# A hybrid decoder layer on one core: the second norm summed across partitions by a product with ones, an earlier GLU input, a square root on ScalarE in the last norm, and sample rows stored in four pieces

## Chip, cores and metric

The kernel runs on one core of one Trainium2 chip. The metric is device time in microseconds (us), the median of several runs. Before the change it is 1431.86 us (three runs, 1431.58 to 1431.98).

## What is computed

One layer of a decoder over 256 prompt positions and 8 x 8 sample positions (320 columns in all), width 2048, all in float32:

```python
h = rms_norm(x, norm_mix)
u, q, k, v, g = split(h @ w_in)
y, s5_re, s5_im = s5_mixer(u, ...)            # complex diagonal scan, then gelu
y = y * sigmoid(y @ w_glu + b_glu)            # the GLU
o, ret_new = retention_chunked(rotary(q), rotary(k), v)
x = x + concat([y, silu(g) * group_norm(o)]) @ w_out
h2 = rms_norm(x, norm_ffn)                    # the second norm
gate, up = split(h2 @ w_ffn_in)
x = x + (silu(gate) * up) @ w_ffn_out
y_prompt, y_sample = rms_norm(x, norm_final)  # the last norm
```

with `rms_norm(x, g) = x * rsqrt(mean(x*x) + 1e-6) * g`. The states of the S5 part and of the retention are outputs too.

## The kernel before

Activations lie transposed: features on the 128 partitions, the N = 320 positions along the free dimension, so x is 16 tiles of 128x320. Every product with weights is made of three products in the fp32r format: weights and activations are split into a high part (a cast) and a low part (the rest), and hi*hi, hi*lo and lo*hi are added in one PSUM bank. `wload` (L132 to L135) fetches 128x1024 weights into `raw` on the SP queue, ACT casts them to `hi`, DVE subtracts to get `lo`; each of the three has three buffers. `gemm` (L145 to L147) runs the three products for each of the contraction's 128-row blocks. Results go to PSUM tiles with the tag "acc", of which there are three.

The order of instructions on PE and POOL is that of the program. Side work (norms, S5 chunks, heads) is written as generators that `spawn` puts on a heap with a due time; `gemm` runs the due ones between two blocks, by a clock `clk.now` that adds up costs written by hand. ACT, DVE and SP are ordered by a scheduler with priorities, except in the last part (`tail_order`), where they keep the program's order too.

The stages in question, in order of time:

- The output projection of the retention half: 16 products `ps_o` of the eight 128-row blocks in `r4a` and `r4b` (hi and lo of each head). `r4a` lies in the buffer "tab" of the S5 pool.
- The GLU: ACT halves the gelu's result `u32` into `yhi` (L1083), DVE takes the rest into `ylo` (L184), and eight products `ps_g` follow; ACT takes their sigmoid (L1098). `yhi` and `ylo` lie in the pool `glp`, which reuses the place of the S5 pool, that of `r4a` among it.
- The output projection of the GLU half (`ps_o2`). DVE adds each result to `x1`; ACT multiplies by the norm's weight into `hhi`, DVE makes `hlo`; squares are summed over the 16 tiles into `acc2` (128x320).
- The second norm, `ffn_norm`, which runs between the first products `ps_fg` of the FFN. `rstd_bcast` sums `acc2` over the partitions with products against a column of ones (positions on partitions, three columns), DVE finds the reciprocal root of the 128x3 numbers in eleven small steps (a guess from the bits, three Newton steps), three products with the identity spread it over all partitions, and ACT copies it from PSUM to `rbc2`. `ffn_in` multiplies each PSUM result by `rbc2`.
- The FFN: 88 products of 16 blocks (`ps_fg`, `ps_fu`) and 61 of 11 blocks (`ps_fo`).
- The tail, from L1336: the last three of the 16 feature tiles are computed with positions on partitions (128 + 128 + 64 rows x 384 features, `ps_t0`, `ps_t1`, `psa` with `psb`), so that the last norm's sum of squares comes from `accum_out` of one ACT Square (`chain`, L1312) plus the sum over the other 13 tiles (`sm3`). For each of the three position tiles `root_of` (L1298) finds the reciprocal root of one column on DVE: a sum, a guess from the bits, and three Newton steps of two instructions each. `bcast` (L1316) spreads it over the partitions with a product on PE, ACT copies it for POOL (`rbt`), DVE and POOL scale the 13 feature tiles (`scale`), ACT scales the 384 token-major features (`tok_out`), and SP or ACT issue the stores. `keep_warm(12)` (L1376) puts twelve unused products of 128x512 on PE between tile 1 and the last `bcast`.

Of the kernel before, what the change touches and what calls it, by code (L numbers as in the profile page):

```python
# [12 lines left out]
F32 = mybir.dt.float32  # L13
# [33 lines left out]
def hybrid_kernel(ctx, tc, xT, w_in, w_in4, w_out, w_glu, w_fi, w_fo, w_fot, gfr, vecs, s5p, bc, x0,  # L47
# [9 lines left out]
    def f(t):  # L57
        return t.bitcast(F32)
# [30 lines left out]
    def spawn(gen, delay=0.0):  # L89
        clk.n += 1  # L90
        heapq.heappush(clk.heap, (clk.now + delay, clk.n, gen))
# [91 lines left out]
    def stt(out, a, s, b, o1, o2):  # L183
        dve.scalar_tensor_tensor(out, a, s, b, o1, o2)  # L184
        return out
# [718 lines left out]
    def do_g(h):  # L904
        ps = proj(11 + 4 * h)
        sg = mp.tile([P, N], F32, name="sg", tag="sg", bufs=2)
        with tc.high_priority(offset=EVAC):
# [4 lines left out]
        run_due()  # L912

    DL = dict(b1=14.2, b2=6.6, scan=17.8, y=10.0, k=8.5, v=6.1,
              o=2.2, u=6.0, c=10.0, n2=2.4, n2b=2.6, nm=0.8)
    T0, PER = 53.6, 32.0


# [133 lines left out]

    rhi, rlo = Cols(), Cols()

    def split_r(t_, h):
        with tc.high_priority(offset=EVAC):
            act.copy(t_[:, 0], retp[:, h])
            tt(t_[:, 1], retp[:, h], f(t_[:, 0]), SUB)
        rhi.a.append(t_[:, 0])
        rlo.a.append(t_[:, 1])  # L1060
# [9 lines left out]
    for h in range(4, H):  # L1070
        while not ("sg" in HS[h] and "gn" in HS[h]):
            advance()
        split_r(r4b[:, h - 4], h)
    while clk.heap:
        advance()
    s5stack.close()
# [8 lines left out]
    for n in range(KT):  # L1085
        if n == 0:
            late = gemm_late("ps_o", lambda n: w_out[n, :, 8:16], 0, 4, 8, rhi, rlo)
        ps = late[n] if n < 2 else gemm("ps_o", w_out[n, :, 8:16], 8, rhi, rlo)
        tt(x1[:, n], x1[:, n], ps, ADD)
    rpool.close()  # L1090
# [44 lines left out]
        return ps_n.tile([P, 512], F32, name=name, tag="n", bufs=2)  # L1135

    def ffn_norm():
        rg = rstd_bcast(hp, acc2, norm_ps, "n2")
        next(rg)
        yield DL["n2b"]  # L1140
        act.copy(rbc2, next(rg))

# [34 lines left out]
    def ffn_in(c):  # L1179
        a = fp.tile([P, 2, FCT, N], F32R, name="ahl", tag="ahl", bufs=2)  # L1180
        for i in range(FCT):
            n = c * FCT + i
            if n == 0:
                spawn(ffn_norm(), DL["n2"])
            pg = gemm("ps_fg", w_fi[2 * n], KT, hhi, hlo)
            g = fp.tile([P, N], F32, name="fg", tag="fg", bufs=2)
            tt(g, pg, rbc2, MUL)
            act.activation(g, g, AF.Silu)
            if n == 0:
                wpool[:] = [wp2, WP2]  # L1190
            pu = gemm("ps_fu", w_fi[2 * n + 1], KT, hhi, hlo)
            u = fp.tile([P, N], F32, name="fu", tag="fu", bufs=2)
            tt(u, pu, rbc2, MUL)
            tt(u, u, g, MUL)
            act.copy(a[:, 0, i], u)
            tt(a[:, 1, i], u, f(a[:, 0, i]), SUB)
            if n >= 2:
                for _ in range(2 if n % 3 else 1):
                    states_step()
        return a  # L1200
# [97 lines left out]
    def root_of(i):  # L1298
        m = TILES[i][1]
        y_, t_, w_ = (a[0:m, i:i + 1] for a in (yy, th, wn))  # L1300
        ts(t_, rs[0:m, i:i + 1], sm3[0:m, i:i + 1], ADD, -0.5, MUL)
        ts(y_.bitcast(I32), t_.bitcast(I32), -0.5, MUL, float(0x1EF759DF), ADD)
        for _ in range(3):
            stt(w_, y_, t_, y_, MUL, MUL)
            stt(y_, w_, 1.5, y_, ADD, MUL)

    def chain(i, ps):

# [25 lines left out]
        q.dma_start(yp_o[i, :, a_:b_] if i < 2 else ys_o[:, a_:b_], outs[i][:, a_:b_])  # L1334

    with tail_order:  # L1336
        ps0 = ps_tok("ps_t0")
        mm3(ps0, 0, P, range(0, 5))
        pss = norm_ps("ps_s3")
# [44 lines left out]
        root_of(2)  # L1384
        pb2 = bcast(2)
        act.copy(rbt[0][:, 0:ms_], pb2[:, 0:ms_])
        scale(dve, 2, 0, 9, pb2)
        store(2, 0, 9)
        scale(pool, 2, 9, NF, rbt[0])
        tok_out(2, ts_o, act)  # L1390
        store(2, 9, NF)


def _host(inp):
# [99 lines left out]
```

## Time and profile before

| | us |
|---|---|
| median of 3 runs | 1431.86 |
| the profiled execution: device time | 1431.66 |
| its span, first to last instruction | 1429.9 |
| PE busy in the span | 1419.3 |
| DVE, ACT, POOL busy | 957.1, 602.9, 126.7 |
| first retention `ps_o` product, first GLU product, first FFN product | 343.9, 400.3, 485.4 |
| first product of the tail, last `bcast` | 1402.8, 1423.6 |

A row of the timeline reads: start, duration, engine, line of the kernel, operation, output<-input, shape, count, and in brackets the idle time of the engine before it and what ended it. A run of equal instructions is merged into one row with its count; products on PE overlap, so the step from one start to the next, not the duration, is what one costs the stream. Engine names with a q (SPq, ACTq) are the sequencers that issue DMAs. The chip's granted clock of TensorE is 0.999 in this execution.

### The profile page before, as it was taken

How to read it: one execution, taken by the hardware profiler on the slowest of the kernel's cores; microseconds unless marked ns; L12 is line 12 of the kernel's file. 1: busy time of each engine (PE TensorE's matmuls, PEld its weight loads, DVE VectorE, ACT ScalarE, POOL GpSimd, SP SyncE). 2: the span in 40 equal slices, each digit the busy share in tenths (PEclk: the TensorE clock that was granted, in tenths of full speed). 3: DMA queues.
4: the chain of work that ended last, by engine and by line, in shares of the span. 5: the costliest groups of instructions: out<-in, count | busy, mean ns of one | idle time of the engine just before them, and what ended most of it. 6: DMA issues, size and time to landing. Idle time of an engine off the chain costs nothing.

```text
span 1429.9 us, 26218 instructions
## 1 busy us (share of the span) xinstructions
PE 1419.3 (99%) x10386; PEld 1407.8 (98%) x10386; DVE 957.1 (67%) x1861; ACT 602.9 (42%) x959; POOL 126.7 (9%) x194
## 2 busy tenths in 40 slices
PE   9999999999999999999999999999999999999998
PEld 8999999999999999999999999999999999999997
DVE  7978887787567646776777545767744677655454
ACT  7645555554355533333333333333333333343452
POOL 7530022110000000000001000000000000000001
PEclk9999999999999999999999999999999999999999
DMA  8555555556444456675766446667445765455542
GB/s 287 173 171 164 162 170 160 168 165 207 161 154 151 158 206 225 221 255 197 250 201 235 136 147 241 235 208 246 159 151 178 256 232 179 156 169 174 161 129 74
DMA packets 102171, 267.07 MB, mean 187 GB/s; under 512 B 27360, under 2 KB 41888, under 8 KB 102048
## 3 DMA queue, kind: packets, MB, share of 16 engines
q1 hardware_dynamic: 101824, 265.04, 56.0%
q8 instruction: 81, 1.33, 0.4%
q10 hardware_dynamic: 224, 0.36, 0.1%
q14 instruction: 42, 0.34, 0.1%
HBM read 254.44 MB, written 10.52 MB: 185 GB/s over the span
## 4 chain that ended last, share of the span: by engine, by line
PE 71%; DVE 0%; issue 0%; POOL 0%; ACT 0%; POOLq 0%
PE ps_fu L146 7%; PE ps_fu L145 7%; PE ps_fu L147 7%; PE ps_fg L146 7%; PE ps_fg L145 7%; PE ps_fg L147 7%; PE ps_fo L146 7%; PE ps_fo L145 7%; PE ps_fo L147 7%; PE ps_o L146 1%; PE ps_o L145 1%; PE ps_o L147 1%; PE ps_t L1295 1%; PE ps_g L146 1%; PE ps_g L147 1%; PE ps_g L145 1%
## 5 line engine op out<-in xcount | busy, mean ns | idle before, releaser
L133 ACT CAST hi<-raw 128x1024 fp32r<-128x1024 f32 (+1 forms) x410 | 397.7, 971 | 681.2 <-PE ps_fg L146 184.2
L135 DVE TENSOR_TENSOR lo<-raw,hi 128x1024 fp32r<-128x1024 f32 (+1 forms) x410 | 463.2, 1130 | 307.3 <-ACT hi L133 304.4
L145 PE MATMUL ps_fg<-hhi,hi 128*128 128x320 f32 x704 | 217.5, 309 | 0.0
L146 PE MATMUL ps_fu<-hlo,hi 128*128 128x320 f32 x704 | 217.4, 309 | 0.0
L146 PE MATMUL ps_fg<-hlo,hi 128*128 128x320 f32 x704 | 217.4, 309 | 0.0
L147 PE MATMUL ps_fg<-hhi,lo 128*128 128x320 f32 x704 | 217.4, 309 | 0.0
L145 PE MATMUL ps_fu<-hhi,hi 128*128 128x320 f32 x704 | 217.4, 309 | 0.0
L147 PE MATMUL ps_fu<-hhi,lo 128*128 128x320 f32 x704 | 217.4, 309 | 0.0
L145 PE MATMUL ps_fo<-ahl,hi 128*128 128x320 f32 x671 | 207.4, 309 | 0.0
L146 PE MATMUL ps_fo<-ahl,hi 128*128 128x320 f32 x671 | 207.2, 309 | 0.0
L147 PE MATMUL ps_fo<-ahl,lo 128*128 128x320 f32 x671 | 207.2, 309 | 0.0
L145 PE MATMUL ps_p<-xhi,hi 128*128 128x320 f32 x560 | 177.3, 317 | 0.0
L147 PE MATMUL ps_p<-xhi,lo 128*128 128x320 f32 x560 | 173.0, 309 | 0.0
L146 PE MATMUL ps_p<-xlo,hi 128*128 128x320 f32 x560 | 172.8, 309 | 0.0
L146 PEld LDWEIGHTS ps_fg<-hlo,hi 128*128 128x128 f32 x704 | 132.4, 188 | 0.0
L145 PEld LDWEIGHTS ps_fg<-hhi,hi 128*128 128x128 f32 x704 | 132.4, 188 | 0.0
L145 PEld LDWEIGHTS ps_fu<-hhi,hi 128*128 128x128 f32 x704 | 132.4, 188 | 0.0
L146 PEld LDWEIGHTS ps_fu<-hlo,hi 128*128 128x128 f32 x704 | 132.4, 188 | 0.0
L147 PEld LDWEIGHTS ps_fu<-hhi,lo 128*128 128x128 f32 x704 | 132.4, 188 | 0.0
L147 PEld LDWEIGHTS ps_fg<-hhi,lo 128*128 128x128 f32 x704 | 132.3, 188 | 0.0
L146 PEld LDWEIGHTS ps_fo<-ahl,hi 128*128 128x128 f32 x671 | 126.2, 188 | 0.0
L145 PEld LDWEIGHTS ps_fo<-ahl,hi 128*128 128x128 f32 x671 | 126.2, 188 | 0.0
(480 smaller groups left out, 2119.7 us busy)
## 6 DMA issues: line engine op xcount, KB each, us to landing
raw<-w_fi SPq DMA_DIRECT2D x176, 512.0 KB, 4.2
raw<-w_in SPq DMA_DIRECT2D x79, 512.0 KB, 4.1
raw<-w_fo SPq DMA_DIRECT2D x61, 512.0 KB, 3.5
raw<-w_out SPq DMA_DIRECT2D x32, 512.0 KB, 3.7
hi<-vd SPq DMA_DIRECT2D x32, 512.0 KB, 5.6
lo<-vd SPq DMA_DIRECT2D x32, 512.0 KB, 5.3
raw<-w_fo SPq DMA_DIRECT2D x61, 192.0 KB, 2.4
rt<-r SPq DMA_DIRECT2D x8, 512.0 KB, 5.8
```

Source lines behind the costliest of these rows:

```text
L133: cast = act.copy(hi[:, :m], raw[:, :m])
L135: last_lo[0] = dve.tensor_tensor(lo[:, :m], raw[:, :m], f(hi[:, :m]), SUB)
L145: pe.matmul(ps, hi, xhi[:, k], start=k == 0, stop=False)
L146: pe.matmul(ps, hi, xlo[:, k], start=False, stop=False)
L147: pe.matmul(ps, lo, xhi[:, k], start=False, stop=k == nk - 1)
L1295: pe.matmul(ps[0:m, 0:TC], a3[:, x_, k, s:s + m], w_[:, k], start=k == 0 and x_ == 0 and w_ is whi, stop=k == FCT - 1 and w_ is wlo)
```

## The change

Four edits.

1. GLU input. The four heads in `r4a` are copied by ACT (two casts of 128x1280) into a new tile `r4c`, which the output projection reads from its fifth result on, so that the last reader of `r4a` comes after four results and not sixteen. The place that `yhi` and `ylo` share with it is free from then.
2. The second norm. `acc2` is split into high and low parts (`shi`, `slo`) on DVE, and two fp32r products with a 128x128 matrix of ones give the sum over the partitions on all partitions at once. DVE then computes the reciprocal root on the whole 128x320, in the same eleven steps, directly into `rbc2`. The six small products and the spreading ones, and ACT's copy, are gone. The due time is 3.4 instead of 2.4 + 2.6.
3. The last norm's root. ACT takes the square root, DVE the reciprocal, and one Newton step of two instructions follows instead of three. A first Sqrt on a column of ones stands at the head of the tail's program.
4. The sample rows. The nine feature tiles that DVE scales are scaled and stored as five and four, and the piece that POOL scales is stored by ACT's queue behind `ts_o`.

```diff
-              o=2.2, u=6.0, c=10.0, n2=2.4, n2b=2.6, nm=0.8)
+              o=2.2, u=6.0, c=10.0, n2=3.4, nm=0.8)
...
+    r4c = rpl.tile([P, 4, 2, N], F32R, name="r4c")
+    with tc.issue_after(last_r[0].ins):
+        for q in range(2):
+            act.copy(r4c[:, 2 * q:2 * q + 2], f(r4a[:, 2 * q:2 * q + 2]))
...
+        if n == 4:
+            rhi.a[0:4], rlo.a[0:4] = ([r4c[:, h, q] for h in range(4)] for q in range(2))
         ps = late[n] if n < 2 else gemm("ps_o", w_out[n, :, 8:16], 8, rhi, rlo)
...
     def ffn_norm():
-        rg = rstd_bcast(hp, acc2, norm_ps, "n2")
-        next(rg)
-        yield DL["n2b"]
-        act.copy(rbc2, next(rg))
+        shi, slo = (fp.tile([P, N], F32R, name=q, tag=q, bufs=2) for q in ("fg", "fu"))
+        ms, w = (hp.tile([P, N], F32, name=q, tag="sqx", bufs=2) for q in ("ms2", "rt2"))
+        with tc.high_priority(offset=2000):
+            dve.tensor_copy(shi, acc2)
+            tt(slo, acc2, f(shi), SUB)
+        yield DL["n2"]
+        ps = norm_ps("ps_r")[:, :N]
+        for i, a in enumerate((shi, slo)):
+            mm(0.15, ps, onesr, a, start=i == 0, stop=i == 1)
+        with tc.high_priority(offset=2000):
+            ts(ms, ps, -0.5 / D, MUL, -0.5 * EPS, ADD)
+            ts(rbc2.bitcast(I32), ms.bitcast(I32), -0.5, MUL, float(0x1EF759DF), ADD)
+            for _ in range(3):
+                tt(w, rbc2, rbc2, MUL)
+                tt(w, w, ms, MUL)
+                stt(rbc2, w, 1.5, rbc2, ADD, MUL)
...
-                spawn(ffn_norm(), DL["n2"])
+                spawn(ffn_norm())
...
     def root_of(i):
...
+        act.activation(w_, rs[0:m, i:i + 1], AF.Sqrt, bias=sm3[0:m, i:i + 1])
         ts(t_, rs[0:m, i:i + 1], sm3[0:m, i:i + 1], ADD, -0.5, MUL)
-        ts(y_.bitcast(I32), t_.bitcast(I32), -0.5, MUL, float(0x1EF759DF), ADD)
-        for _ in range(3):
-            stt(w_, y_, t_, y_, MUL, MUL)
-            stt(y_, w_, 1.5, y_, ADD, MUL)
+        dve.reciprocal(y_, w_)
+        stt(w_, y_, t_, y_, MUL, MUL)
+        stt(y_, w_, 1.5, y_, ADD, MUL)
...
     with tail_order:
+        act.activation(wn[:, 0:1], ones[:, 0:1], AF.Sqrt)
...
-        scale(dve, 2, 0, 9, pb2)
-        store(2, 0, 9)
+        scale(dve, 2, 0, 5, pb2)
+        store(2, 0, 5)
         scale(pool, 2, 9, NF, rbt[0])
         tok_out(2, ts_o, act)
-        store(2, 9, NF)
+        scale(dve, 2, 5, 9, pb2)
+        store(2, 5, 9)
+        store(2, 9, NF, act)
```

How this moves instructions, at three places. First DVE around the GLU's input, before (`ps_o` results are added to `x_4853`, which is `x1`; `u_119` is `u32`; `lo` splits weights):

```order
L135 TENSOR_TENSOR lo<-raw,hi 128x1024
L184 SCALAR_TENSOR_TENSOR ylo<-u_119,yhi 128x320 x5
L180 TENSOR_TENSOR x_4853<-x_4853,ps_o 128x320
L135 TENSOR_TENSOR lo<-raw,hi 128x1024
L184 SCALAR_TENSOR_TENSOR ylo<-u_119,yhi 128x320 x3
L135 TENSOR_TENSOR lo<-raw,hi 128x1024
L184 SCALAR_TENSOR_TENSOR sgl<-u_119,sgl 128x320
```

and after, where `y_4898` is the last S5 chunk's gelu input:

```order
L180 TENSOR_TENSOR y_4898<-y_4898,y_4897 128x320
L184 SCALAR_TENSOR_TENSOR u_119<-y_4898,y_4897 128x320
L180 TENSOR_TENSOR x_4853<-x_4853,ps_o 128x320
L135 TENSOR_TENSOR lo<-raw,hi 128x1024
L184 SCALAR_TENSOR_TENSOR ylo<-u_119,yhi 128x320 x7
L135 TENSOR_TENSOR lo<-raw,hi 128x1024
L184 SCALAR_TENSOR_TENSOR ylo<-u_119,yhi 128x320
L180 TENSOR_TENSOR x_4853<-x_4853,ps_o 128x320 x2
```

The eight `ylo` steps now follow the last S5 chunk, seven results of the projection earlier, and two additions of projection results wait behind them.

On ACT at the start of the projection and at the same place, after (before, `r4c` is absent, and the eight `yhi` stand as five and three on either side of the last weight cast but one ahead of the first sigmoid, L1098):

```order
L1079 CAST r4c<-r4a 128x1280 x2
L133 CAST hi<-raw 128x1024 x8
L689 ACTIVATE y_4898<-y_4897 128x320
L690 ACTIVATE y_4898<-y_4898,ones 128x320
L692 ACTIVATE y_4898<-y_4898 128x320
L133 CAST hi<-raw 128x1024
L1089 ACTIVATE yhi<-u_119 128x320 x8
L133 CAST hi<-raw 128x1024 x8
L1106 ACT_TABLE_LOAD
```

The two copies stand ahead of eight weight casts, the eight `yhi` directly behind the last gelu.

Second, DVE in the second norm, before (`acc_5783` is `acc2`, `ms`, `ry` and `rt` are the 128x3 tiles of the root):

```order
L180 TENSOR_TENSOR acc_5783<-acc_5783,sqx 128x320
L176 TENSOR_SCALAR ms<-ps_r 128x3
L176 TENSOR_SCALAR ry<-ms 128x3
L180 TENSOR_TENSOR rt<-ry 128x3
L180 TENSOR_TENSOR rt<-rt,ms 128x3
L184 SCALAR_TENSOR_TENSOR ry<-rt,ry 128x3
```

and after (`fg` and `fu` are the tiles of `shi` and `slo`, `ms_6415` and `rt_6416` the wide ones of the root, `rbc_5787` is `rbc2`):

```order
L180 TENSOR_TENSOR acc_5786<-acc_5786,sqx 128x320
L1149 CAST fg<-acc_5786 128x320
L180 TENSOR_TENSOR fu<-acc_5786,fg 128x320
L135 TENSOR_TENSOR lo<-raw,hi 128x1024
L176 TENSOR_SCALAR ms_6415<-ps_r 128x320
L135 TENSOR_TENSOR lo<-raw,hi 128x1024
L176 TENSOR_SCALAR rbc_5787<-ms_6415 128x320
L180 TENSOR_TENSOR rt_6416<-rbc_5787 128x320
L135 TENSOR_TENSOR lo<-raw,hi 128x1024
L180 TENSOR_TENSOR rt_6416<-rt_6416,ms_6415 128x320
L184 SCALAR_TENSOR_TENSOR rbc_5787<-rt_6416,rbc_5787 128x320
```

Of four splits of weights one stands ahead of the wide steps and two among the first of them; the last stands behind four more wide steps and ahead of the final two. The first multiplication by `rbc2` comes after all eleven. On PE the two products with ones stand behind 30 of the first 48 FFN products, the six sums of before stood behind 21 and the six spreading products behind 42.

Third, DVE at the last position tile, before:

```order
L180 TENSOR_TENSOR hi<-ps_b,ahl 64x384
L1330 TENSOR_TENSOR ahl<-x_4853,ps_b_15908 128x384
L176 TENSOR_SCALAR ahl<-ahl 64x1 x2
L184 SCALAR_TENSOR_TENSOR ahl<-ahl 64x1 x6
L1330 TENSOR_TENSOR ahl<-x_4853,ps_b_15952 128x576
```

and after:

```order
L180 TENSOR_TENSOR hi<-ps_b,ahl 64x384
L1350 TENSOR_TENSOR ahl<-x_4853,ps_b_15903 128x384
L176 TENSOR_SCALAR ahl<-ahl 64x1
L1323 RECIPROCAL ahl<-ahl 64x1
L184 SCALAR_TENSOR_TENSOR ahl<-ahl 64x1 x2
L1350 TENSOR_TENSOR ahl<-x_4853,ps_b_15944 128x320
L1350 TENSOR_TENSOR ahl<-x_4853,ps_b_15944 128x256
```

Of eight one-column steps on DVE four are left; the Sqrt is on ACT between the Square and the copy of `bcast`'s result. The table load for the Sqrt stands on ACT in the last FFN products, between the scaling of the last norm's weights (L1281 before) and that of its row form (L1282); no other load follows it.

More of the change, by code (lines that the diff above doesn't have):

```diff
@@ L1053, in hybrid_kernel @@
     rhi, rlo = Cols(), Cols()
+    last_r = [None]
     def split_r(t_, h):
         with tc.high_priority(offset=EVAC):
-            act.copy(t_[:, 0], retp[:, h])
+            last_r[0] = act.copy(t_[:, 0], retp[:, h])
             tt(t_[:, 1], retp[:, h], f(t_[:, 0]), SUB)
```

## The prediction, made before the changed kernel was run

> **What bounds the kernel now.** I read the page first, then the list of waits of PE, then the timeline of PE around each wait.
>
> ```profile
> PE 1419.3 (99%) x10386; PEld 1407.8 (98%) x10386; DVE 957.1 (67%) x1861; ACT 602.9 (42%) x959; POOL 126.7 (9%) x194
> ```
>
> PE is busy 99% of the span: the time is the stream of products, and only three things can shorten it: fewer products, fewer holes in their stream, and a shorter way from the last product to the end. All four edits lie at such places. The waits of PE name two of them:
>
> ```profile
> PE ps_b L1319 <- DVE ahl L184: 0.8, 2, 0.5
> ...
> PE ps_g L146 <- DVE ylo L184: 0.3, 1, 0.3
> ```
>
> The columns are the sum, the count and the longest: 0.8 us for the root in the tail, 0.3 for the GLU's `ylo`. These figures are taken from modelled ends of products, so I measure holes by steps between starts. "About what this kernel's measurement can tell" is 0.2%, 2.86 us.
>
> **Edit 1, the GLU input.** PE's timeline at the sixth block of the first GLU product:
>
> ```profile
> 402.54 0.31 PE L145 MATMUL ps_g<-yhi,hi 128*128 128x320 f32 x1
> 403.18 0.41 PE L146 MATMUL ps_g<-ylo,hi 128*128 128x320 f32 x1 [0.34 <-DVE ylo L184]
> 403.43 0.30 PE L147 MATMUL ps_g<-yhi,lo 128*128 128x320 f32 x1
> ```
>
> A product of 320 columns costs the stream 0.147 us (21 of them between the first two rows of the next fence: 3.08 / 21). Here two steps take 0.64 and 0.25: the hole is 0.89 - 0.29 = 0.60 us. With `ylo` made seven results of the projection earlier it closes: **-0.60**. What pays for it: two copies of 128x1280 and eight `yhi` that move on ACT, eight `ylo` that move on DVE.
>
> The copies: no row has that shape; the weight cast of 128x1024 in the next fence takes 1.05, and by its length 1280 columns take 1.3 each, 2.5 together with some overlap. They fit the idle 2.52 ahead of the cast that follows them:
>
> ```profile
> 349.40 1.05 ACT L133 CAST hi<-raw 128x1024 fp32r<-128x1024 f32 x1 [2.52 <-PE ps_o L164]
> ```
>
> Should they take longer, that cast (of the fourth result's weights) has cover: the product that needs it starts at 343.9 + 3 x 3.52 = 354.5 (24 steps of 0.147 are 3.52), and the cast and DVE's split are done 2.3 us after 349.4, so 2.7 us of lateness cost nothing. The eight `yhi` and `ylo` are some 3 to 4 us each, moved within a stage in which DVE and ACT have time:
>
> ```profile
> 343.90:400.30 56.40, 56.40 (x387) 56.34 (x385) 33.46 (x49) 21.54 (x30) 0.00 (x0) 1.00 0.60 205
> ```
>
> The columns are the stretch, then busy us of PE, PEld, DVE (33.46 of 56.40) and ACT (21.54). The two additions queued behind `ylo` come 3 us late, and their PSUM banks are wanted again two results (7.0 us) after they are full. So I price the cover at 0, with a bound of 0.6 above: then the hole has only moved.
>
> **Edit 2, the second norm.** PE's timeline from the first FFN product:
>
> ```profile
> 485.41 0.31 PE L145 MATMUL ps_fg<-hhi,hi 128*128 128x320 f32 x1
> ...
> 488.49 0.72 PE L104 MATMUL ps_r<-ones,acc 128*128 128x1 f32 x6
> 489.08 0.39 PE L145 MATMUL ps_fg<-hhi,hi 128*128 128x320 f32 x1
> 489.31 0.31 PE L146 MATMUL ps_fg<-hlo,hi 128*128 128x320 f32 x1
> ...
> 492.09 0.31 PE L147 MATMUL ps_fg<-hhi,lo 128*128 128x320 f32 x1
> 492.46 0.93 PE L104 MATMUL ps_r<-ident,ry 128*128 128x128 f32 x6
> 493.15 0.39 PE L145 MATMUL ps_fg<-hhi,hi 128*128 128x320 f32 x1
> 493.38 0.31 PE L146 MATMUL ps_fg<-hlo,hi 128*128 128x320 f32 x1
> ```
>
> The sums cost 489.31 - 488.49 - 0.147 = 0.67. The spreading products, the wait for `ry` ahead of them included, cost 493.38 - 492.09 - 2 x 0.147 = 1.00. Both go (1.67); two fp32r products of 320 columns come, 0.29: **-1.38**. Do they wait? The rows of DVE:
>
> ```profile
> 487.20 0.48 DVE L180 TENSOR_TENSOR acc<-acc,sqx 128x320 f32<-128x320 f32 x1
> ...
> 494.95 0.48 DVE L180 TENSOR_TENSOR fg<-ps_fg,rbc 128x320 f32<-128x320 f32 x1
> ```
>
> `acc2` is ready at 487.68; the cast and the subtraction, two steps of at most 0.49, end at 488.7. PE reaches the new products after 30 steps, 485.41 + 4.41 = 489.82: 1.1 us to spare.
>
> The root itself grows from eleven steps of 0.2 to eleven of up to 0.49, some 5.4 us, with three weight splits among them (1.2 each), and the last of those waits for this cast, which waits for PE:
>
> ```profile
> 497.73 1.05 ACT L133 CAST hi<-raw 128x1024 fp32r<-128x1024 f32 x1 [1.79 <-PE ps_fu L146]
> ```
>
> So `rbc2` is ready at about 500, not 493.9, and the first result is multiplied some 5 us later than at 494.95. What hides it: its bank is wanted by the fourth FFN product, three products of 7.04 us (48 steps) and 0.29 after 485.41, at 506.8, so 6 us are left; the splits that stand between the wide steps feed products that start 3 us or more after they end. ACT's copy leaves too, but ACT waits for nothing here. Cover gone would mean a wait of PE at 506.8; I price it at 0, bounds 0 and +1.
>
> **Edit 3, the root in the tail.** PE's timeline of the tail:
>
> ```profile
> 1412.27 0.34 PE L1295 MATMUL ps_t<-hlo,ahl 128*128 128x384 f32 x1
> 1412.57 0.49 PE L1319 MATMUL ps_b<-ident,ahl 128*128 128x128 f32 x2
> ...
> 1417.40 0.86 PE L1365 MATMUL ps_b<-hlo,ahl 128*64 128x384 f32 x4
> 1418.75 0.49 PE L1319 MATMUL ps_b<-ident,ahl 128*128 128x128 f32 x2 [0.48 <-DVE ahl L184]
> ...
> 1420.28 2.93 PE L118 MATMUL warm_ps<-ones 128*128 128x512 f32 x12
> 1423.55 0.40 PE L1319 MATMUL ps_b<-ident,ahl 64*128 64x64 f32 x2 [0.34 <-DVE ahl L184]
> ```
>
> A 384-column product steps by (0.86 - 0.34) / 3 = 0.173. So PE could have issued the first `bcast` at 1412.44 (0.13 lost), the second at 1417.40 + 4 x 0.173 = 1418.09 (0.66 lost). At the third the twelve warm products end, as modelled, 0.34 before it; with the overlap that the second shows (0.66 lost where 0.48 is listed) about 0.5 is lost. What the chain ahead of a `bcast` costs:
>
> ```profile
> 1416.72 0.19 ACT L1312 ACTIVATION_READ_ACCUMULATOR ahl<-hi 128x1 f32 x1
> 1417.60 0.48 ACT L1363 COPY ahl<-ps_a 64x384 f32<-64x384 f32 x1 [0.69 <-PE ps_a L1361]
> ```
>
> ```profile
> 1417.38 1.31 DVE L184 SCALAR_TENSOR_TENSOR ahl<-ahl 128x1 f32<-128x1 f32 x6
> ...
> 1420.48 0.55 DVE L180 TENSOR_TENSOR hi<-ps_b,ahl 64x384 f32<-64x384 f32 x1
> ```
>
> From the end of the sum of squares (1416.91) to the `bcast` (1418.75): 1.84. After: Sqrt, reciprocal and two steps of 1.31 / 6 = 0.22, with some 0.12 for four hand-overs, 0.56 and the two unknowns. The nearest rows for them:
>
> ```profile
> L922 ACT ACTIVATE warm<-ones 128x1 f32<-128x1 f32 x1 | 0.2, 203 | 0.0
> ```
>
> ```profile
> L432 DVE RECIPROCAL scrt<-scrt 128x32 f32<-128x32 f32 x1 | 0.4, 354 | 0.0
> ```
>
> The Sqrt lies between 0.20 (one column) and 0.48 (the copy of 384), the reciprocal between 0.20 (a one-column step) and 0.35 (32 columns); I take 0.25 and 0.20, both being one column. The chain is then 1.0, shorter by 0.8 (0.5 at the dear ends). Does PE collect it? First `bcast`: 0.13, all that PE lost. Second: 0.66 + 0.13 = 0.79 earlier, if the chain gives 0.66, which it does by 0.15. Then tile 2's sum (the row at 1420.48) waits for DVE, not PE: ACT's copy of `psa` at 1417.60 moves by 0.13 only, two additions and a scaling follow it on DVE, and the sum starts about 0.63 earlier. The chain ends 0.63 + 0.8 = 1.4 earlier, but PE is at the twelve warm products, which end 0.79 earlier, and so the last `bcast` comes 0.79 + 0.5 = about 1.25 earlier: **-1.25**. The warm products set it, with 0.15 to spare, so the dear ends cost 0.2 at most; the bounds are -0.9 and -1.4. Behind the Sqrt on ACT stands only the copy of `psa`, which waits for PE longer; behind the reciprocal on DVE stand tile 2's additions, which wait for that copy.
>
> The load of the Sqrt table costs what the sigmoid's does, 1.28 in the first row below, and falls into the hole of the last row, 2.42 in which ACT waits for a transfer:
>
> ```profile
> 405.57 1.28 ACT L1098 ACT_TABLE_LOAD   x1
> 406.86 0.53 ACT L1098 ACTIVATE sgl<-ps_g,vec 128x320 f32<-128x320 f32 x1
> ```
>
> ```profile
> 1342.56 0.53 ACT L1282 ACTIVATE ahl<-ahl 128x384 f32<-128x384 f32 x1 [2.42 <-DMA ahl<-gfr]
> ```
>
> 1.28 + 0.2 of the first Sqrt fit: 0.
>
> **Edit 4, the sample stores.** The rows of the two issuing queues, and of the transfers (KB each, time from issue to landing):
>
> ```profile
> 1424.78 0.56 ACTq L1326 DMA_DIRECT2D ts_o<-hi  x1
> 1425.01 1.06 SPq L1334 DMA_DIRECT2D ys_o<-ahl  x2
> ```
>
> ```profile
> rs_o<-raw SPq DMA_DIRECT2D x8, 512.0 KB, 6.7
> ...
> ys_o<-ahl SPq DMA_DIRECT2D x1, 128.0 KB, 3.4
> ts_o<-hi ACTq DMA_DIRECT2D x1, 96.0 KB, 3.0
> ```
>
> Before, the last piece is issued at about 1425.45 and lands 3.4 later, at 1428.8, 1.1 ahead of the span's end. After, by the same clock: five tiles scaled and issued 0.3 earlier (1424.7; 256 elements fewer, and 384 take 0.55 in the row at 1420.48), four at about 1425.15, and ACT's piece behind `ts_o`'s issue at about 1425.35. The last issue comes 0.1 earlier, and half of SP's bytes start 0.3 earlier: **-0.2**, bounds -0.5 and +0.4 (a fourth completion, a second issue of 0.5 on ACT).
>
> **Sum.** -0.60 - 1.38 - 1.25 - 0.2 = -3.43. The profiled execution is 1431.66, 0.20 under the median of 1431.86, and 1.76 longer than its span; I subtract from the median: **1428.4 us**, 0.24% faster.
>
> **The rivals.**
>
> *A hidden step shows, and the gain is within 0.2%.* A copy into `r4c` that takes the time of two casts and more, or a wide root step in the second norm that pushes a split past its product, puts a wait of 0.6 to 1 back; or the tail's stores land 0.5 later. Against it: every cover above is over a microsecond, except the tail's 0.15. For it: the forecast clears 2.86 by only 0.6. Time 1429.2.
>
> *The table set.* If Square is not served by the set that holds Sqrt, each tile's Sqrt is preceded by a load. Each chain becomes 2.3 instead of 1.84: 0.5 lost at each of the first two `bcast`, and at tile 2 another 0.3 for loading Square's set back (ACT is idle 1.01 there, below) and 0.5 for the Sqrt. With 0.1 to 0.2 back from the stores the tail ends 1.6 later: 1431.86 - 1.98 + 1.6 = 1431.5.
>
> ```profile
> 1421.06 0.53 ACT L1379 ACTIVATE ahl<-hi 64x384 f32<-64x384 f32 x1 [1.01 <-DVE hi L180]
> ```
>
> Against it: the program holds a single load for Sqrt, and Square and Copy have run behind the loads for Silu and Sigmoid without one of their own. The Trainium skill, "ScalarE: Activation LUTs", section "Table sets: the hidden batching unit", advises to group calls by table set, which speaks against mixing Sqrt with Square in one chain; it calls copy and identity members of every set and does not list Square. The Trainium skill's section "What ACT_TABLE_LOAD costs" gives 2.66 us for a switch (1283 ns of load and a drain of 1380); the load agrees with the row of this trace, where the sigmoid starts 1.29 after the load with no drain between. By the Trainium skill's price this rival would end near 1437.
>
> *Slower, by the stores.* The last 128 KB piece is now behind another on ACT's queue. A store of 512 KB lands after 6.7 us in this trace, under load. If the new last piece took that long from its issue (1425.35 - 1.25 + 6.7 = 1430.8, against 1428.8), the end would come 2.0 later than before and undo edits 1 and 2: 1431.9. From a landing of 6.6 on, the change is no gain, and past 9.5 us it is slower by 0.2%. Against it: the piece is a quarter of that size, and nothing else is under way.
>
> *No effect of edit 1.* If the scheduler's earlier `yhi` waited for something else that shares the place (the S5 outputs), the hole stays: 1429.0. The table of moved rows speaks against it.
>
> **Chances.** The forecast 0.68; a hidden step shows 0.2; edit 1 void 0.05; the table set 0.03; the stores 0.04. The 80% range takes the bounds of the four terms (-3.9 to -2.1, the latter with one cover gone): 1427.9 to 1429.8. Faster by over 0.2% is below 1429.0: 0.62 of the forecast's 0.68, and 0.06 of the second case, 0.68. Slower by over 0.2% takes both of the last two at their dear ends: 0.03. Within: 0.29.
>
> **What would show it.** In the changed profile: no wait of `ps_g` on `ylo`, and steps of 0.147 through the first GLU product; two products `ps_r` 4.4 us behind the first FFN product, 0.29 in all, and no wait at the fourth; the second `bcast` directly behind four `ps_b` products; the last one directly behind the twelve warm products, no longer listed as waiting for DVE; one Sqrt of about 0.25 and a reciprocal of about 0.2 in each chain; a last landing 1.4 to 1.5 earlier relative to the tail's first product. I am wrong if PE waits for `lo` after 343.9, 376 or 494, if a second table load stands in the tail, or if ACT's store lands over 4 us after its issue.

## The result, and the profile after

The changed kernel takes 1428.14 us (median of 9 runs, 1427.61 to 1428.76); the kernel before, run beside it, 1431.77 (9 runs, 1430.89 to 1432.89). The ratio is 0.9974, with a 95% interval of 0.9966 to 0.9983: 3.6 us faster, forecast 3.43. The interval ends at 0.17%, so the whole times alone leave open whether the gain is over 0.2%; the stages below make it 3.67 us, 0.26%. The span of the profiled execution went from 1429.9 to 1426.0.

The first row is the page's busy time of the changed kernel, in the form shown for the kernel before; the fence behind it is the whole list of waits of PE.

```profile
PE 1416.9 (99%) x10376; PEld 1406.4 (99%) x10376; DVE 958.0 (67%) x1852; ACT 606.4 (43%) x965; POOL 124.6 (9%) x194
```

```profile
PE warm_ps L118 <- POOL ones L64: 1.1, 1, 1.1
PE pss L104 <- POOL ksp L882: 0.9, 1, 0.9
PE py L953 <- ACT hi L943: 0.6, 1, 0.6
PE py L104 <- DMA toe<-toe: 0.5, 1, 0.5
PE py L953 <- DVE xhi L180: 0.3, 1, 0.3
```

The two waits that the prediction started from, `ps_b` on DVE and `ps_g` on DVE, are gone, and no wait stands in their place: all five rows left belong to the first 344 us, which no edit touches. PE's busy time fell by 2.4 us, with ten products fewer; the rest of the gain is time in which PE waited, or behind its last product, and 0.19 is an earlier first `ps_o` (343.91 and 343.72), which is no gain of the edits.

Where the time went is best read in stages, each from the start of one product of PE to the start of another, so that one execution's early or late start does not matter (us; the last column ends at the span's end, 1429.88 and 1426.03; the expectations further down have it from the span as rounded on the page, 6.35 and 5.92):

| | first `ps_g` to first `ps_fg` (edit 1) | first `ps_fg` to first `ps_fu` (edit 2) | first tail product to last `bcast` (edit 3) | last `bcast` to the end (edit 4) |
|---|---|---|---|---|
| before | 85.07 | 8.70 | 20.70 | 6.33 |
| after | 84.48 | 7.35 | 19.35 | 5.95 |
| difference | -0.59 | -1.35 | -1.35 | -0.38 |
| forecast | -0.60 | -1.38 | -1.25 | -0.2 |

The two long stages between are the same within 0.07 (56.43 and 56.50 from `ps_o` to `ps_g`, 908.74 and 908.68 from `ps_fu` to the tail). The four differences make -3.67.

**Edit 1.** ACT's timeline of the changed kernel at the start of the projection and behind the last gelu, then the group of `ps_g`'s products that read `ylo` (shortest, middle and longest duration in ns):

```profile
346.62 2.42 ACT L1079 CAST r4c<-r4a 128x1280 fp32r<-128x1280 f32 x2
349.24 1.05 ACT L133 CAST hi<-raw 128x1024 fp32r<-128x1024 f32 x1 [0.20 <-PE ps_o L164]
...
376.59 2.99 ACT L1089 ACTIVATE yhi<-u 128x320 fp32r<-128x320 f32 x8
```

```profile
L146 PE MATMUL ps_g<-ylo,hi x64: 309/309/309, 400.4 to 428.1; 128*128 128x320 f32 x64
```

The copies take 2.42 for both, and the weight cast behind them still waits for PE, 0.20 in the bracket where 2.52 stood: they fill the idle time, and the cast starts 5.52 us behind the first `ps_o`, against 5.49 before. All 64 `ylo` products now have the same duration; the longest took 412 ns before.

**Edit 2.** PE and then DVE of the changed kernel around the second norm:

```profile
488.95 0.31 PE L147 MATMUL ps_fg<-hhi,lo 128*128 128x320 f32 x1
489.11 0.31 PE L104 MATMUL ps_r<-fg,ones 128*128 128x320 f32 x1
489.25 0.31 PE L104 MATMUL ps_r<-fu,ones 128*128 128x320 f32 x1
489.40 0.32 PE L145 MATMUL ps_fg<-hhi,hi 128*128 128x320 f32 x1
```

```profile
487.44 0.49 DVE L180 TENSOR_TENSOR fu<-acc,fg 128x320 fp32r<-128x320 f32 x1
...
489.60 0.49 DVE L176 TENSOR_SCALAR ms<-ps_r 128x320 f32<-128x320 f32 x1 [0.53 <-PE ps_r L104]
...
498.36 0.49 DVE L184 SCALAR_TENSOR_TENSOR rbc<-rt,rbc 128x320 f32<-128x320 f32 x1
498.89 0.49 DVE L180 TENSOR_TENSOR fg<-ps_fg,rbc 128x320 f32<-128x320 f32 x1
```

Two products with ones stand in the stream at its usual step, 4.41 us behind the first FFN product (484.70). Their second input was ready at 487.93, 1.2 before PE came. The root on DVE ends at 498.85, 14.15 us behind the first product, and no product waits for it.

**Edit 3.** The tail of the changed kernel on PE, then the chain of the second tile on ACT and DVE, and the last step of the third tile's chain:

```profile
1410.35 0.38 PE L1339 MATMUL ps_b<-ident,ahl 128*128 128x128 f32 x2
...
1415.09 0.86 PE L1386 MATMUL ps_b<-hlo,ahl 128*64 128x384 f32 x4
1415.78 0.39 PE L1339 MATMUL ps_b<-ident,ahl 128*128 128x128 f32 x2
...
1417.22 2.92 PE L118 MATMUL warm_ps<-ones 128*128 128x512 f32 x12
1420.08 0.43 PE L1339 MATMUL ps_b<-ident,ahl 64*128 64x64 f32 x2
```

```profile
1414.40 0.18 ACT L1332 ACTIVATION_READ_ACCUMULATOR ahl<-hi 128x1 f32 x1
1414.62 0.29 ACT L1321 ACTIVATE ahl<-ahl 128x1 f32<-128x1 f32 x1
```

```profile
1414.95 0.16 DVE L1323 RECIPROCAL ahl<-ahl 128x1 f32<-128x1 f32 x1
1415.14 0.41 DVE L184 SCALAR_TENSOR_TENSOR ahl<-ahl 128x1 f32<-128x1 f32 x2
...
1419.33 0.40 DVE L184 SCALAR_TENSOR_TENSOR ahl<-ahl 64x1 f32<-64x1 f32 x2
```

The second `bcast` stands directly behind the four `ps_b` products (4 x 0.173 = 0.69), the third directly behind the twelve warm products; neither has a bracket any more. The Sqrt takes 0.29 and the reciprocal 0.16, and from the end of the sum of squares (1414.58) to the end of the last step (1415.55) it is 0.97. The old chain needed 1.84 to the `bcast` itself, of which 0.06 lay behind the last step (1418.69 to 1418.75), so 1.78 is the figure to compare: 0.81 less, forecast 0.8. The table load lies in ACT's hole, of which 0.88 is left:

```profile
1338.07 1.28 ACT L1357 ACT_TABLE_LOAD   x1
1339.36 0.20 ACT L1357 ACTIVATE ahl<-ones 128x1 f32<-128x1 f32 x1
1340.45 0.53 ACT L1302 ACTIVATE ahl<-ahl 128x384 f32<-128x384 f32 x1 [0.88 <-DMA ahl<-gfr]
```

**Edit 4.** The issues of the sample rows on the two queues of the changed kernel:

```profile
1421.30 0.55 ACTq L1346 DMA_DIRECT2D ts_o<-hi  x1
1421.94 0.54 ACTq L1354 DMA_DIRECT2D ys_o<-ahl  x1
```

```profile
1421.30 0.81 SPq L1354 DMA_DIRECT2D ys_o<-ahl  x2
```

The first feature-major piece is issued 1.22 us behind the last `bcast` (1.46 before), the last issue ends 2.40 behind it (2.5 before). The stage is 0.38 shorter, more than the earlier last issue gives; the store experiments below tell why.

### The profile page after: what moved, and what is told of

It is laid out like the page before. It is cut to its first block, busy times and chain, and to the rows that moved or that the text cites. A ratio compares the mean times of both kernels' runs of the same rounds, so it can differ in the third digit from the quotient of the medians.

```text
span 1426.0 us, 26198 instructions
## 1 busy us (share of the span) xinstructions
PE 1416.9 (99%) x10376; PEld 1406.4 (99%) x10376; DVE 958.0 (67%) x1852; ACT 606.4 (43%) x965; POOL 124.6 (9%) x194
## 4 chain that ended last, share of the span: by engine, by line
PE 76%; DVE 1%; issue 0%; ACT 0%; DMA 0%; SPq 0%; DVEq 0%; ACTq 0%
PE ps_fu L146 7%; PE ps_fg L146 7%; PE ps_fg L145 7%; PE ps_fu L145 7%; PE ps_fg L147 7%; PE ps_fu L147 7%; PE ps_fo L146 7%; PE ps_fo L145 7%; PE ps_fo L147 7%; PE ps_o L145 2%; PE ps_o L147 2%; PE ps_o L146 2%; PE ps_t L1315 1%; PE ps_g L147 1%; PE ps_g L145 1%; PE ps_g L146 1%
```

## The experiments

Eleven more kernels ran, and the changed one once more. Whole times of one kernel scatter by 1 to 3 us, and a single edit is worth 0.4 to 1.4, so the single edits are judged by the stages and the whole times are given beside them.

### Each edit alone

Four kernels are the kernel before with one edit each:

```diff
# edit 1 alone
+    last_r = [None]
...
-            act.copy(t_[:, 0], retp[:, h])
+            last_r[0] = act.copy(t_[:, 0], retp[:, h])
...
+    r4c = rpl.tile([P, 4, 2, N], F32R, name="r4c")
+    with tc.issue_after(last_r[0].ins):
+        for q in range(2):
+            act.copy(r4c[:, 2 * q:2 * q + 2], f(r4a[:, 2 * q:2 * q + 2]))
...
+        if n == 4:
+            rhi.a[0:4], rlo.a[0:4] = ([r4c[:, h, q] for h in range(4)] for q in range(2))
# edit 2 alone: ffn_norm and its due times as in the change
-        rg = rstd_bcast(hp, acc2, norm_ps, "n2")
...
+        for i, a in enumerate((shi, slo)):
+            mm(0.15, ps, onesr, a, start=i == 0, stop=i == 1)
...
# edit 3 alone: root_of and the first Sqrt as in the change
...
+        act.activation(w_, rs[0:m, i:i + 1], AF.Sqrt, bias=sm3[0:m, i:i + 1])
...
+        dve.reciprocal(y_, w_)
...
# edit 4 alone
-        scale(dve, 2, 0, 9, pb2)
-        store(2, 0, 9)
+        scale(dve, 2, 0, 5, pb2)
+        store(2, 0, 5)
...
-        store(2, 9, NF)
+        scale(dve, 2, 5, 9, pb2)
+        store(2, 5, 9)
+        store(2, 9, NF, act)
```

Edit 1: 

> Edit 1 alone, on the kernel before. Theory (PE's stream sets the time, each edit closes its own hole): no wait of ps_g on ylo, the stretch from the first GLU product to the first FFN product 0.60 us shorter (85.07 to 84.47), nothing else moved: 0.6 us faster, some 1431.2. Rival (the hole only moves: the copies or the late additions make PE wait elsewhere in the projection): same time as before, with a new wait of ps_o between 343 and 400 us.

Edit 2: 

> Edit 2 alone, on the kernel before. Theory: first ps_fg to first ps_fu 7.34 us instead of 8.70, no later wait of PE: 1.38 us faster, some 1430.4. Rival (the wide root on DVE holds back weight splits or the PSUM bank, and PE pays part of it later): under 0.8 us faster, with a wait of ps_fu or ps_fg between 492 and 510 us.

Edit 3: 

> Edit 3 alone, on the kernel before. Theory: from the tail's first product to the last bcast 19.35 us instead of 20.70 (1.35 less: 0.1, 0.65 and 0.6 at the three), and the end follows one to one: 1.3 us faster, some 1430.5. Rival (the end is set by the transfers of tile 1's stores or by POOL, not by the last root): the last bcast is 1.35 earlier but the span only 0.5 or less.

Edit 4: 

> Edit 4 alone, on the kernel before. Theory: last bcast where it was, first sample piece issued 0.3 us earlier, last one 0.1 earlier, landing 0.2 to 0.4 earlier: span 0.2 to 0.4 us shorter. Rival A (completion is fixed by the number of transfers): no gain or a loss up to 0.4. Rival B (this edit carries the gain that the sum did not foresee): 0.5 us or more.

| | edit 1 stage | edit 2 stage | edit 3 stage | edit 4 stage | first `ps_o` at | median, runs | ratio to before, 95% interval |
|---|---|---|---|---|---|---|---|
| before | 85.07 | 8.70 | 20.70 | 6.33 | 343.91 | 1431.97, 33 | |
| edit 1 alone | **84.48** | 8.70 | 20.70 | 6.31 | 343.35 | 1431.54, 11 | 0.9996 [0.9987, 1.0005] |
| edit 2 alone | 85.07 | **7.34** | 20.73 | 6.32 | 344.98 | 1430.96, 11 | 0.9993 [0.9984, 1.0002] |
| edit 3 alone | 85.07 | 8.70 | **19.33** | 6.32 | 344.66 | 1430.66, 11 | 0.9989 [0.9980, 0.9998] |
| edit 4 alone | 85.08 | 8.70 | 20.70 | **5.94** | 345.05 | 1431.93, 11 | 0.9999 [0.9990, 1.0007] |

Each edit moves its own stage by what it moves in the whole change, and no other stage of the table by more than 0.03. The four gains, 0.59, 1.36, 1.37 and 0.39, add up to 3.71 (3.67 in the whole change): they are independent. The stretch from the first `ps_o` to the first `ps_g` is not in the table; with edit 1 alone it is 56.58, against 56.43 before. The excess is time lost between `ps_o` products 3.6 to 3.8 us behind the first, up to 0.16 in one profile. Five of the ten profiles with `r4c` show none of it, and the kernel before has 0.06 of it, so it is at most a small part of what edit 1 gains. The whole times alone would not have told this: three of four intervals hold 1, because each edit is worth less than the 1.7 us by which the first `ps_o` moves between executions.

### Which of the two sets the last `bcast`: nine warm products instead of twelve

```diff
-        keep_warm(12)
+        keep_warm(9)
```

> The changed kernel with 9 instead of 12 warming products of 128x512 behind the second tile's sum product. In the changed kernel the last scalar product of the tail (1420.08) stands right behind the last warming product, and its input, scaled by ACT and DVE, was ready at 1419.73. If the warming products set the end there, as the prediction's working says, three fewer (about 0.24 each) uncover the chain of the last tile: the stage from the first tail product to the last scalar product goes from 19.35 to about 19.0, and the end comes 0.35 earlier. Rival: the chain itself, not the warming products, sets the end, and the stage stays at 19.35. Second rival: without the products PE's granted clock falls and the last products get longer by more than the 0.35, so the stage is 19.4 or more.

PE of this kernel, then DVE's last step ahead of the third `bcast`:

```profile
1418.67 2.25 PE L118 MATMUL warm_ps<-ones 128*128 128x512 f32 x9
1421.32 0.40 PE L1339 MATMUL ps_b<-ident,ahl 64*128 64x64 f32 x2 [0.40 <-DVE ahl L184]
```

```profile
1420.77 0.40 DVE L184 SCALAR_TENSOR_TENSOR ahl<-ahl 64x1 f32<-64x1 f32 x2
```

The stage went from 19.35 to 19.14, with the granted clock still at 1.00. Now the `bcast` waits for the chain, whose last step ends at 1421.17; the hand-over to PE takes another 0.15. So the twelve products do set the end in the changed kernel, by 0.21. I had expected 0.35, from the end of the chain without the hand-over. The whole time, 1428.52 (ratio 0.9975 [0.9967, 0.9984]), can't show 0.2.

### The cover of the wide root: eight Newton steps instead of three

```diff
-            for _ in range(3):
+            for _ in range(8):
                 tt(w, rbc2, rbc2, MUL)
```

> The changed kernel with 8 Newton steps for the second norm's root instead of 3: 15 more wide DVE instructions of about 0.52, 7.9 us in all, behind the sums and ahead of the scale of fg and fu; the values are the same but for rounding. It measures the cover that the prediction gave the root (the two bounds were 4.9 by the weight tile's low half on DVE and 6.7 by the PSUM bank of ps_fg that PE wants back). If that cover is right, PE waits 1.2 to 3 us behind the first product of the second weight product, and the time rises by that much against the changed kernel: 1429.3 to 1431.2. Rival: the root is on PE's path already and the whole 7.9 shows (1436). Second rival: DVE has more room than that and nothing shows (1428.1).

DVE at the end of the root, then PE at the fourth FFN product, which wants the bank back that the first result fills, then PE's clock by stretches (in front of the DMA share, the granted clock):

```profile
511.16 0.49 DVE L184 SCALAR_TENSOR_TENSOR rbc<-rt,rbc 128x320 f32<-128x320 f32 x1
511.69 0.49 DVE L180 TENSOR_TENSOR fg<-ps_fg,rbc 128x320 f32<-128x320 f32 x1
```

```profile
507.85 0.31 PE L147 MATMUL ps_fg<-hhi,lo 128*128 128x320 f32 x1
512.32 0.61 PE L145 MATMUL ps_fu<-hhi,hi 128*128 128x320 f32 x1 [4.16 <-DVE fg L180]
512.73 0.47 PE L146 MATMUL ps_fu<-hlo,hi 128*128 128x320 f32 x1
...
515.53 0.31 PE L145 MATMUL ps_fu<-hhi,hi 128*128 128x320 f32 x1
```

```profile
508.00:512.30 4.30, 0.16 (x2) 0.01 (x1) 4.13 (x9) 2.42 (x3) 0.00 (x0) 0.96 0.93 312
512.30:515.00 2.70, 2.68 (x10) 2.70 (x11) 1.79 (x4) 1.24 (x3) 1.91 (x1) 0.50 1.02 408
515.00:516.00 1.00, 1.00 (x8) 1.00 (x7) 0.00 (x0) 0.00 (x0) 1.00 (x1) 0.82 0.43 172
```

The kernel takes 1434.88 (ratio 1.0021 [1.0012, 1.0030]), outside all three expectations, yet the cover itself came out as predicted. The root ends 25.07 behind the first FFN product (486.58) instead of 14.15: 10.92 later, not 7.9, because three more weight splits of DVE get between the added steps. PE starts the product 4.32 late (512.32 against 507.85 + 0.147). The cover is the difference, 10.92 - 4.32 = 6.6 us; the prediction had 6.8 (500 against 506.8). Then came what I had not counted: after that idle time the granted clock is 0.50, and from 512.32 to 515.53 twelve products take 3.21 instead of 1.76, another 1.45. The stretch from the first `ps_fu` to the tail is 5.79 longer, 914.47 instead of 908.68, which is 4.32 + 1.45 within 0.02. The Trainium skill, "TensorE: Matmul & The Clock Gate", section "Part 1: The HAM clock gate", says that the array falls to half its clock after an idle window of about 3.4 us and comes back after about as long under load; here an idle 4.3 us cost 3.2 us at half clock, so the trace agrees.

### What a reloaded table set would have cost

A Silu stands ahead of each tile's Square: one line in `chain`, which serves the first two tiles, and one for the third:

```diff
+        act.activation(wn[0:m, 2:3], ones[0:m, 0:1], AF.Silu)
...
+        act.activation(wn[0:ms_, 0:1], ones[0:ms_, 0:1], AF.Silu)
         act.activation(sqj[0:ms_], x_, AF.Square, accum_out=rs[0:ms_, 2:3])
```

> The changed kernel with one more one-column Silu of a constant on ACT ahead of the sum of squares of the second and of the third tile, so that a table load for Silu and one for Sqrt stand in each of these tiles' chains; the values computed stay the same. It makes the prediction's rival of a reloaded table set true on purpose and prices it. By the row of the load that the trace shows (1.28, the next activation 1.29 behind its start) each tile gets the Sqrt load between its sum and its root, and the Silu load ahead of its Square: the stage from the first tail product to the last scalar product goes from 19.35 to about 22.4, and the time to about 1431.2. If a drain of 1.4 stands behind every load as well, the stage goes to about 26 and the time to about 1435. Rival: the loads are hidden beside the warming products and the stage stays within 0.3 of 19.35.

ACT in the second tile's chain, then PE's second `bcast`:

```profile
1414.69 0.18 ACT L1333 ACTIVATION_READ_ACCUMULATOR ahl<-hi 128x1 f32 x1
1414.90 1.28 ACT L1321 ACT_TABLE_LOAD   x1
1416.19 0.29 ACT L1321 ACTIVATE ahl<-ahl 128x1 f32<-128x1 f32 x1
```

```profile
1417.18 0.49 PE L1340 MATMUL ps_b<-ident,ahl 128*128 128x128 f32 x2 [0.95 <-DVE ahl L184]
```

The stage to the last `bcast` is 22.56: 3.21 longer than with the change, where the rows of the load alone gave 3.05. The first tile's chain, which the expectation leaves out, pays too: against the kernel before, the three `bcast` come 0.49, 0.96 and 1.86 later, where the prediction's rival had 0.5, 1.0 and 1.8. The kernel takes 1432.06 (ratio 1.0000 [0.9990, 1.0009]): by whole times nothing of the gain is left, by the four stages (84.48, 7.35, 22.56, 5.86) 0.55 us of it. The prediction's price for that rival, 1431.5, was 0.36 under the kernel before. The Trainium skill, "ScalarE: Activation LUTs", section "What ACT_TABLE_LOAD costs", adds a drain of 1380 ns to each load; here the activation starts 1.29 behind the start of a load of 1.28, so no run shows a drain, and its price for the rival, 1437, was too high. Without the added Silu, Square runs beside Sqrt without a load, as the single load of the changed kernel's tail shows.

### Why the stores gained more

The forecast for edit 4 was -0.2, the measured gain 0.38 in the whole change and 0.39 alone. Edit 4 does two things, which these kernels part: the first leaves POOL's piece on ACT's queue but stores DVE's nine tiles in one piece, the second keeps DVE's two pieces but issues POOL's on SP.

```diff
# one piece by DVE
-        scale(dve, 2, 0, 5, pb2)
-        store(2, 0, 5)
+        scale(dve, 2, 0, 9, pb2)
+        store(2, 0, 9)
...
-        scale(dve, 2, 5, 9, pb2)
-        store(2, 5, 9)
# three pieces on SP
-        store(2, 9, NF, act)
+        store(2, 9, NF)
```

One piece by DVE: 

> The changed kernel with DVE's nine feature tiles of the sample rows scaled and stored in one piece again (288 KB on SP), while the piece that POOL scales stays on ACT's queue behind the token-major store. It takes edit 4 apart: the stage from the last scalar product to the end is 6.35 without the edit and 5.92 to 5.96 with it. If the gain comes from issuing POOL's piece on ACT's queue instead of behind DVE's piece on SP, the stage stays at about 5.95. If it comes from the smaller and earlier pieces of DVE, it goes back to about 6.3.

Three pieces on SP: 

> The changed kernel with all three feature-major pieces of the sample rows (160, 128 and 128 KB) on SP's queue, DVE's scaling still in two steps of five and four tiles. If the gain of edit 4 comes from ACT's queue, the third issue on SP (about 0.45 behind the second) gives it back and the stage from the last scalar product to the end is about 6.3 instead of 5.92. If it comes from the smaller pieces, the stage stays at about 5.95.

Each ran once (1428.87 and 1428.50 us; the kernel before, once beside them, 1432.57). The stage is 6.34 with one piece and 5.83 with three on SP. The whole gain is the earlier small piece. Taking ACT's queue for the last one gains nothing: with it the stage is 5.86 to 5.95 in the six profiles that have all of edit 4 and the old order of the tail, so the 0.03 to 0.12 that SP seems to save is about as large as their scatter. The reason shows in the traffic from 1.7 to 2.3 us and then to 4.3 us behind the last `bcast` (the last two figures are the mean busy share of the DMA engines and GB/s). Before, and after:

```profile
1425.25:1425.85 0.60, 0.00 (x0) 0.00 (x0) 0.00 (x0) 0.00 (x0) 0.00 (x0) 1.00 0.00 0
1425.85:1427.85 2.00, 0.00 (x0) 0.00 (x0) 0.00 (x0) 0.00 (x0) 0.00 (x0) 0.54 0.86 234
```

```profile
1421.78:1422.38 0.60, 0.00 (x0) 0.00 (x0) 0.00 (x0) 0.00 (x0) 0.00 (x0) 1.00 0.39 132
1422.38:1424.38 2.00, 0.00 (x0) 0.00 (x0) 0.00 (x0) 0.00 (x0) 0.00 (x0) 1.00 0.82 221
```

The same first stretch, 1.7 to 2.3 us behind the last `bcast`, with one piece by DVE, and with three pieces on SP:

```profile
1422.45:1423.05 0.60, 0.00 (x0) 0.00 (x0) 0.00 (x0) 0.00 (x0) 0.00 (x0) 1.00 0.00 0
```

```profile
1422.59:1423.19 0.60, 0.00 (x0) 0.00 (x0) 0.00 (x0) 0.00 (x0) 0.00 (x0) 1.00 0.38 130
```

In the two microseconds that follow, the DMA engines are busy for 80% or more (0.86 before and with one piece, 0.82 after, 0.80 with three on SP), and nearly all 512 KB (416 of `ys_o`, 96 of `ts_o`) go. The two kernels with a small first piece move bytes in the first stretch, the two without move none. By the trace's packets the first byte moves 2.44 us behind the last `bcast` before and with one piece, 2.06 after and with three on SP; from there to the end it is 3.8 to 3.9 in all four. The end of the last issue does not order them: 2.52 before, 2.42 with one piece, 2.40 after, 2.53 with three on SP. So the end is set by when the first bytes move, not by when the last piece is issued.

One thing stays open. SP's first piece is issued 0.24 earlier than before, but its bytes start 0.78 earlier: 0.84 behind the issue, where the 288 KB piece needed 1.38. No run here parts the size of the piece from the time of its issue.

### A faster tail

The tail's remaining slack suggests a better order: nine warm products; on DVE the third tile's sum ahead of the second tile's output scaling, and its root ahead of the last part of that scaling; on ACT the third tile's scaling ahead of the last copy.

```diff
-        scale(dve, 1, 0, 5, pb1)
...
-        store(1, 0, 5)
-        keep_warm(12)
+        keep_warm(9)
         x_, g_ = xo[0][0:ms_], xg[0][0:ms_]
         tt(x_, psb[0:ms_, 0:TC], xt[0:ms_, 2], ADD)
         act.activation(sqj[0:ms_], x_, AF.Square, accum_out=rs[0:ms_, 2:3])
-        scale(dve, 1, 10, NF, pb1)
+        scale(dve, 1, 0, 5, pb1)
+        store(1, 0, 5)
         store(1, 5, 10)
-        store(1, 10, NF)
...
         root_of(2)
+        scale(dve, 1, 10, NF, pb1)
+        store(1, 10, NF)
+        act.mul(xo[0][0:ms_], xg[0][0:ms_], yy[0:ms_, 2:3])
         pb2 = bcast(2)
...
-        tok_out(2, ts_o, act)
+        act.dma_start(ts_o, xo[0][0:ms_])
```

> The changed kernel with 9 instead of 12 warming products, the last tile's sum and root placed on DVE ahead of the second tile's output scaling, and the last tile's sample scaling placed on ACT ahead of the last copy. If the last scalar product is set by the warming products and then by the last tile's chain behind DVE's scaling of the tile before, the stage from the first tail product to the last scalar product goes from 19.35 to about 18.9, and the stage from there to the end from 5.92 to about 5.55: 0.8 us faster than the changed kernel, about 1427.3. Rival: the output scaling of the second tile, now later, reaches the end itself, and the last stage grows by what the first one loses: 1428.1.

The stages are 18.99 and 5.45, 0.86 us less than in the changed kernel, as expected. The `bcast` again waits for the chain, whose last step ends at 1420.82; the hand-over of 0.15 is that of the kernel with nine warm products:

```profile
1420.97 0.40 PE L1339 MATMUL ps_b<-ident,ahl 64*128 64x64 f32 x2 [0.24 <-DVE ahl L184]
```

A last kernel also puts POOL's sample piece on SP (`store(2, 9, NF)`), and the changed kernel ran beside it.

> The changed kernel with 9 warming products, the last tile's sum and root ahead of the second tile's output scaling on DVE, the sample scaling ahead of the last copy on ACT, and all three feature-major sample pieces on SP. The runs before gave 18.99 for the stage from the first tail product to the last scalar product (19.35 in the changed kernel) and 5.43 for the stage to the end with ACT's queue taking POOL's piece; three pieces on SP took 0.11 off that stage by themselves. If both add up, the last stage is about 5.3 and the kernel is 0.95 us faster than the changed one run beside it. Rival: the second tile's late store still moves on the DMA engines when the sample pieces start, so that the order of the queues makes no difference, and the stage stays at 5.43.

The changed kernel again: 

> The changed kernel itself, on the same chip as the variant above, so that the two are compared run beside run: 0.9974 of the kernel before in the first series, 19.35 and 5.92 in the two stages of the tail. The start ahead of 344 us, which no edit touches, may differ by up to 2 us between the two profiles.

Its stages are 18.98 and 5.57: the first as before, the second 0.12 longer instead of 0.1 shorter, so nearer to the rival. The three issues on SP follow those of the second tile:

```profile
1418.43 1.67 SPq L1354 DMA_DIRECT2D yp_o<-ahl  x3
1420.61 1.33 SPq L1354 DMA_DIRECT2D ys_o<-ahl  x3
```

The last one ends 2.53 behind the `bcast` (1419.41); with the piece on ACT's queue the last of all issues ended 2.02 behind it. That may be why: the last stores of the second tile are issued up to 0.7 behind the `bcast` here, so the DMA engines are in use already, and the last issue may count again. But 0.12 between two single profiles is not much more than the 0.09 by which this stage scatters, and no run parts the two.

| | median, runs | ratio to before, 95% interval |
|---|---|---|
| better order | 1427.60, 6 | 0.9969 [0.9958, 0.9981] |
| and all pieces on SP | 1428.27, 6 | 0.9970 [0.9959, 0.9982] |
| the changed kernel again | 1428.51, 11 | 0.9977 [0.9968, 0.9986] |

By its stages the better order is the fastest that ran: 0.8 to 0.9 us less than the changed kernel, 0.1 less than with all pieces on SP. The ratios lie on the same side, but their intervals overlap those of the changed kernel. The changed kernel's second series repeats its stages: 19.34 and 5.89.

## Why the prediction was right, step by step

- *Edit 1, -0.60: measured -0.59.* The hole closed, and the copies (2.42 together, estimated 2.5) fit the idle time with the 0.20 left. The late additions showed in no listed wait of PE behind 344 us.
- *Edit 2, -1.38: measured -1.35.* Both halves held: six small products and the spreading cost 1.67, two wide ones 0.29. The root ended 14.15 behind the first FFN product, estimated 14.6, and the lengthened root showed that the cover was 6.6 us.
- *Edit 3, -1.25: measured -1.35.* The Sqrt took 0.29 (I took 0.25), the reciprocal 0.16 (0.20), the chain 0.97 to its last step (1.0). The three `bcast` came earlier by 0.10, 0.85 and 1.35, forecast 0.13, 0.79 and 1.25. The missing 0.1 is the second `bcast`: the wait there cost PE 0.75, not 0.66. The claim that the warm products set the third with 0.15 to spare was measured at 0.21.
- *Edit 4, -0.2: measured -0.4, within its bounds.* This term was mis-sized. The step that failed is the one that followed the last piece: "The last issue comes 0.1 earlier". It did come 0.1 earlier (2.52 and 2.40 behind the `bcast`), but the end does not follow it: with the DMA engines busy for 80% or more behind the first bytes, the 0.38 by which these come earlier is the gain. The prediction saw the earlier first piece ("half of SP's bytes start 0.3 earlier") and gave it only part of its weight; SP's bytes in fact start 0.78 earlier.
- *The rivals.* No hidden step shows in the list of waits. The table set was not reloaded; priced on the chip, it would have taken 3.1 of the 3.7. The last piece did not hold up the end, as the stage behind the last `bcast` got shorter; its own landing is not in the trace of the changed kernel, and in the kernel with one piece by DVE the same store landed 3.4 after its issue, under the 4 that would have shown the forecast wrong. Edit 1 was not void.

The terms measured make 3.7, forecast 3.43; the difference is the stores' 0.2 and the root's 0.1. Both misses lie on the same side, so the sum did not come out by errors that cancel.

## What to carry to other kernels

Where one engine is busy 99% of the time, look for holes in its stream by the steps between starts, price each edit at its own hole, and look for the next thing that is late; wide, slow work on an idle engine is free as long as its result is wanted later than it is ready. For the end of a kernel, ask when the first byte of the last stores moves, not when the last store is issued: where the DMA engines stay busy from the first byte to the last, as here, the end moves by as much as the first byte does. And judge small edits by a stage between two starts of the same engine, since whole times can scatter by more than an edit is worth.

## What was not expected of the hardware

- The first `ps_o`, ahead of which every kernel here is the same, started between 343.35 and 345.63 in 14 profiles. PE's wait for POOL's `ksp` was 0.5 to 0.9 in seven of them, and six of these started before 344.0; it was 1.2 to 1.6 in the other seven, and all of these started after 344.4. What makes POOL late in some executions stays open.
- An idle time of 4.3 us on PE (eight Newton steps) cost 1.45 us more, in products at half clock, than the wait itself.
- A table load of 1.28 us is followed by its activation after 1.29 to 1.30, at five loads in the tail of the kernel with reloads.
